# Temporaries placed 64 bytes ahead of the ring's tiles modulo 256, and the cross attention's split keys kept in temporaries

## The chip, the cores and the metric

The kernel runs on one core of a Trainium2 chip. The metric is the device time of one execution in microseconds (us), the median of several. TensorE (PE in the rows, PEld for its weight loads), VectorE (DVE), ScalarE (ACT), GpSimd (POOL) and SyncE (SP) each work through a queue of their own, in the order in which the program was written.

## What is computed

Two transformer-like blocks run one after the other on 256 positions of width 1024, each of depth 2, all in fp32. The part that the change touches by name is the cross attention of the first block:

```python
def memory_cross_attention(x, mem, xa_q, xa_kv, xa_o):
    q = (x @ xa_q).reshape(b, s, XA_HEADS, XA_DIM) * (XA_DIM ** -0.5)   # 4 heads of 256
    k, v = jnp.split(mem @ xa_kv, 2, axis=-1)
    ...
    p = jax.nn.softmax(jnp.einsum('bqhd,bkhd->bhqk', q, k), axis=-1)
    o = jnp.einsum('bhqk,bkhd->bqhd', p, v).reshape(b, s, D_MODEL)
    return o @ xa_o

def first_block(x, mem, ...):
    x = layer_norm(x)
    for l in range(DEPTH):
        x = layer_norm(alpha * x + hybrid_mixer(x, ...))
        x = layer_norm(alpha * x + memory_cross_attention(x, mem, ...))
        x = layer_norm(alpha * x + conv_ffn(x, ...))
```

The hybrid mixer holds a differential attention, a neighbourhood attention and a short convolution; the second block holds two gated feed-forward parts and a mixer with two more attentions, a pooling and a long convolution.

## The kernel before

Each fp32 operand of a large product is split into a high and a low part of type fp32r, and a product is the sum of three matmuls: high by high, high by low, low by high (`mm3`, `half_A`, `group_B`, `run_BK`). Weights come from HBM in pieces of 128 x 1024 by SP's queue into `stg` (5 buffers); ACT casts the high part into `wh` (8 buffers, L313), DVE subtracts the low part into `wl` (7 buffers, L327). Activations stand transposed in `xT`, the memory in `memT`, its keys in `KT`.

Everything that a stage makes goes into one of two pools of tiles with 2048 bytes in each partition: `ring` (23 buffers: split activations, queries, values, gains of the norms) and `tmp` (8 buffers: softmax rows, their transposes, gated products). Each pool hands out its buffers in turn, and the first writer of a buffer waits until all readers of the tile that stood there before are done. The order of instructions on each engine is the order of the Python code (`manual_schedule`); nothing reorders it.

In `cross`, `q(h)` makes the queries of head h with 48 matmuls of 256 columns (`chunk_A`, L392 to L394), splits them into two tiles and splits that head's keys out of `KT` into two more (`split_to`, ACT L522 and DVE L523). Behind it `unit(h)` issues the 12 matmuls of the scores (L1225), the softmax (`attend`, L751 to L790), its transposes (L771), the split of the transposed rows into two temporaries, and the 12 matmuls with the values (L1233):

```python
            t = [[self.ring([128, 2, 256], F32R) for _ in range(2)] for _ in range(2)]
            self.split_to(t[0][0], t[0][1], ps, scale=1.0 / 16.0)
            self.split_to(t[1][0], t[1][1], KT[:, 2 * h:2 * h + 2, :])
```

Where a tile starts inside a partition follows from the pools' order in `__init__`, `first` and `second`. In the built program the start addresses modulo 256 are: `stg`, `wh`, `wl`, `xn`, `ident`, `ring` and `tmp` at 128; `xT`, `memT` and `KT` at 64 (for `memT` and `KT` by the 192 bytes of `gap1` ahead of them). In a row of the trace a matmul's names stand as out<-moving,stationary: `acc<-xT,wh` streams `xT` against weights loaded from `wh`, `tp<-ring,ring` at L1225 streams keys against queries, `tp<-tmp,ring` at L1233 streams softmax rows against values, `tp<-ident,tmp` is a transpose that loads the temporary and streams the identity.

Of the kernel before, what the change touches and what calls it, by code (L numbers as in the profile page):

```python
# [11 lines left out]
F32 = mybir.dt.float32  # L12
F32R = mybir.dt.float32r
# [222 lines left out]
class Gen:  # L236
    def __init__(self, nc, tc, T, ctx):
        self.nc, self.tc, self.T, self.ctx = nc, tc, T, ctx
        P = lambda name, bufs, **k: ctx.enter_context(tc.tile_pool(name=name, bufs=bufs, **k))
        self.p_stg = P("stg", 5)  # L240
        self.p_hl = P("wh", NHL)
        self.p_wl = P("wl", NHL - 1)
        self.p_one = P("one", 1)
        self.p_xT = P("xT", 1)

        P("gap", 1).tile([128, 16], F32, name="gap")
        self.p_ring = P("ring", 23)
        self.p_tmp = P("tmp", 8)
        self.p_sm = P("sm", 24)
        PS = bass.MemoryType.PSUM  # L250
        self.p_acc = P("acc", 4, space=PS)
        self.p_tp = P("tp", 4, space=PS)
        self.used = 0
        self.n = 0
        self.cur = 0
        self.n_dma = 0
        self.n_h = 0
        self.n_l = 0
        self.stg = {}
        self.hl = {}  # L260
        self.lead = 4
        self.floor = None
        self.sides = []
        self.later = []
        self.early = []
# [578 lines left out]
    def first(self, ctx):  # L844
        nc, T = self.nc, self.T
        pf = ctx.enter_context(self.tc.tile_pool(name="first", bufs=1))
        pna = ctx.enter_context(self.tc.tile_pool(name="na", bufs=2))
        pf.tile([128, 48], F32, name="gap1")
        memT = pf.tile([128, 8, 2, 256], F32R, name="memT")
        KT = pf.tile([128, 8, 256], F32, name="KT")  # L850
        make_identity(nc, self.ident)
        nc.gpsimd.memset(self.mhalf, -0.5)
        self.idle_work(WARM)
        mraw = [self.ring([128, 2, 256]) for _ in range(4)]
        for j in range(2):
            nc.scalar.dma_start(mraw[0][:, j, :], T["memT"][:, j, :])
        self.dma_w()
        for k in range(1, 4):
            nc.sync.dma_start(mraw[k], T["memT"][:, 2 * k:2 * k + 2, :])
            self.dma_w()  # L860

        def load_x(t):
            for c in range(2):
                nc.sync.dma_start(self.halves(t)[c], T["x"][t * 128:t * 128 + 128, c * 512:c * 512 + 512])

        load_x(0)
        self.dma_w()
        g0, b0 = self.bcast_rows(T["emb_ln_g"], D, nc.sync), self.bcast_rows(T["emb_ln_b"], D, nc.sync)
        load_x(1)
        self.trig = pf.tile([128, 4, 2, 8], F32, name="trig")  # L870
        self.posf = pf.tile([128, 2], F32, name="posf")
        self.posi = pf.tile([128, 2], I32, name="posi")
        self.memT, self.KT = memT, KT

        nc.vector.tensor_copy(memT[:, 0, 0, :], mraw[0][:, 0, :])
        self.split_h()
        nc.vector.tensor_sub(memT[:, 0, 1, :], mraw[0][:, 0, :], memT[:, 0, 0, :].bitcast(F32))
        self.split_l()
        self.split_to(memT[:, 1, 0, :], memT[:, 1, 1, :], mraw[0][:, 1, :])
        for k in range(1, 4):  # L880
            self.split_to(memT[:, 2 * k:2 * k + 2, 0, :], memT[:, 2 * k:2 * k + 2, 1, :], mraw[k])
            self.pump(k, 0)

        def emb(t):
            list(self.ln_chain(self.halves(t), g0, b0))

        self.lead = 2
        xT = self.new_xT()

        def after(i):  # L890
            if i == 1:
                emb(0)
                nc.sync.dma_start(self.c1, T["c1"])
                nc.sync.dma_start(self.cols, T["cols"])
                self.lamr = self.ring([128, 2, 4, 64])
                nc.sync.dma_start(self.lamr, T["lamr"].partition_broadcast(128))
                nc.sync.dma_start(self.subg, T["subln_g"].partition_broadcast(128))
                nc.sync.dma_start(self.posi, T["pos"])
            if i == 3:
                self.transpose_in(0, self.halves(0), xT)  # L900
                self.lead = 3
            if i == 5:
                emb(1)
                self.lead = 4

        self.xk_first(after)
        tr1 = self.turn1(self.halves(1), xT)
        for l in range(DEPTH):
            xT, tr1 = self.mixer1(l, xT, tr1, pna)
            xT, tr1 = self.cross(l, xT, tr1)  # L910
            if l == 0:
                self.sides.append(self.small_setup2())
            xT, tr1 = self.ffn1(l, xT, tr1)
        return xT, tr1
# [295 lines left out]
    def cross(self, l, xT, tr1):  # L1210
        nc, T = self.nc, self.T
        x = lambda k: xT[:, k, :, :]
        V, KT = [], self.KT
        qT, oT = [], []
        kok = [0, 1, 2, 3] if l == 0 else []

        def unit(h):

            passes = [(a, b, f) for a, b in ((0, 0), (0, 1), (1, 0)) for f in range(2)]

            def A(sc):
                q, k = qT[h]
                for t in range(2):
                    for n, (a, b, f) in enumerate(passes):
                        nc.tensor.matmul(sc[0][:, t, :], q[a][:, f, t * 128:t * 128 + 128], k[b][:, f, :], start=(n == 0),  # L1225
                                         stop=(n == 5))

            def C(PT, o):
                o3 = o.rearrange("p (a b) -> p a b", a=2)
                for f in range(2):  # L1230
                    vc = (h % 2) * 256 + f * 128
                    for n, (a, b, c) in enumerate(passes):
                        nc.tensor.matmul(o3[:, f, :], V[h // 2][c][a][:, vc:vc + 128],  # L1233
                                         PT[0][b][:, c, :, :].rearrange("p a b -> p (a b)"), start=(n == 0), stop=(n == 5))

            def post(o):
                o3 = o.rearrange("p (a b) -> p a b", a=2)
                for f in range(2):
                    p = self.pair()
                    self.split_to(p[:, 0, :], p[:, 1, :], o3[:, f, :])  # L1240
                    oT.append(p)

            return dict(A=A, C=C, post=post, nk=[256, 256], bias=None, norm=self.norm_plain, nb=1, split=True,
                        ready=lambda: len(qT) > h and len(kok) > h, ready_c=lambda: len(vok) > h // 2)

        side = self.attend([unit(h) for h in range(4)])

        self.sides.append(side)
        vok = []

        def q(h):
            ps = self.chunk_A(("A", "xa_q", l, h), x)
            t = [[self.ring([128, 2, 256], F32R) for _ in range(2)] for _ in range(2)]
            self.split_to(t[0][0], t[0][1], ps, scale=1.0 / 16.0)
            self.split_to(t[1][0], t[1][1], KT[:, 2 * h:2 * h + 2, :])
            self.defer(1, lambda: qT.append(t))

        def v(g):
            V.append(self.xv(l, g))
            self.defer(1, lambda: vok.append(g))  # L1260

        if l == 0:
            v(0)
            tr1()
            for h in range(4):
                q(h)
        else:
            self.xk(l, (0, 1), kok)
            tr1()
            q(0)  # L1270
            q(1)
            self.xk(l, (2,), kok)
            q(2)
            v(0)
            self.xk(l, (3,), kok)
            q(3)
        v(1)

        def get(i):
            while len(oT) <= i:  # L1280
                self.step()
            return oT[i]

        return self.ln_end([("BK", "xa_o", l, k) for k in range(4)], get, T["ln_g"][l, 1], T["ln_b"][l, 1])
# [81 lines left out]
    def swiglu(self, l, which, xT, tr1, gap, final=False):  # L1366
# [21 lines left out]
        for j in range(2, NFF):  # L1388
            ps = self.chunk_A(("UG", n, l, j), x, pool=self.acc if j < NFF - 2 else self.tp)
            if j == 2:  # L1390
                first()
            s, p = self.tmp([128, 256]), self.pair()
            nc.scalar.activation(s, ps[:, 1, :], AF.Silu)  # L1393
            nc.vector.tensor_tensor(s, ps[:, 0, :], s, op=ALU.mult)  # L1394
            self.split_to(p[:, 0, :], p[:, 1, :], s)
            hT.append(p)
# [251 lines left out]
```

## Time and profile before

| | |
|---|---|
| median of 3 runs | 2019.42 us (2018.86 to 2019.86) |
| profiled execution, its own time | 2019.2 us |
| its span, first to last instruction | 2017.4 us |
| PE busy | 1995.2 us, 99% |
| PEld busy | 1825.7 us, 90% |
| DVE busy | 1321.1 us, 65% |
| ACT busy | 1094.0 us, 54% |
| POOL busy | 97.1 us, 5% |
| mean granted TensorE clock | 0.997 of full |

Busy time is the union of an engine's instructions. Matmuls overlap in the rows (one begins while the one before is still draining), so the sum of their durations is more than the span; what one matmul costs is the distance from its start to the next start. The 1.8 us between the span and the execution's own time lie outside all instructions.

### The profile page before, as it was taken

The numbers are of one execution on the slowest core, as the hardware profiler recorded it, in microseconds if no ns is written. First come the engines' busy times: TensorE is split into PE (matmuls) and PEld (weight loads), VectorE is DVE, ScalarE is ACT, GpSimd is POOL, SyncE is SP. The second block draws the span as 40 slices with busy tenths as digits, with TensorE's granted clock in tenths as the row PEclk, the third lists the DMA queues.
The fourth block names the chain that finished last, engine by engine and source line by source line (L and its number), as shares of the span: only waits on it lengthen the run. The fifth ranks groups of instructions, "written<-read, shape, count | busy, mean of one in ns | idle before, by whom it ended". The sixth has DMA issues, their size and how long they took to land.

```text
span 2017.4 us, 35071 instructions
## 1 busy us (share of the span) xinstructions
PE 1995.2 (99%) x14178; PEld 1825.7 (90%) x14178; DVE 1321.1 (65%) x2036; ACT 1094.0 (54%) x1806; POOL 97.1 (5%) x142
## 2 busy tenths in 40 slices
PE   9999999999999999999999999999999999999997
PEld 8899989899888999989987998879998998879996
DVE  6776676787577657667766655776555655676553
ACT  5757446465375754546553544575444554575552
POOL 2100000000020000000001000100000000110000
PEclk9999999999999999999999999999999999999999
DMA  8554655466564564645674666555664666445661
GB/s 293 185 165 157 205 194 166 146 216 209 192 204 139 170 212 164 200 156 183 199 245 160 211 197 227 157 161 180 192 228 147 212 195 225 162 153 183 196 224 67
DMA packets 105667, 376.91 MB, mean 187 GB/s; under 512 B 12576, under 2 KB 13088, under 8 KB 105376
## 3 DMA queue, kind: packets, MB, share of 16 engines
q1 hardware_dynamic: 99792, 357.59, 53.5%
q0 software_dynamic: 5136, 16.29, 2.9%
q8 instruction: 111, 1.82, 0.4%
q10 hardware_dynamic: 576, 0.79, 0.1%
q14 instruction: 52, 0.43, 0.1%
HBM read 372.49 MB, written 1.05 MB: 185 GB/s over the span
## 4 chain that ended last, share of the span: by engine, by line
PE 92%; DVE 4%; DMA 1%; issue 1%; ACT 1%; POOL 1%; POOLq 0%; SPq 0%; DVEq 0%; ACTq 0%
PE acc L392 16%; PE acc L394 16%; PE acc L393 16%; PE acc L487 6%; PE acc L485 6%; PE acc L486 6%; PE acc L510 4%; PE acc L430 3%; PE acc L432 3%; PE acc L431 3%; PE acc L452 2%; PE acc L459 1%; PE acc L454 1%; PE tp L392 1%; PE tp L393 1%
## 5 line engine op out<-in xcount | busy, mean ns | idle before, releaser
L327 DVE TENSOR_TENSOR wl<-stg,wh 128x1024 fp32r<-128x1024 f32 (+1 forms) x671 | 801.1, 1221 | 158.6 <-PE acc L486 114.3
L313 ACT CAST wh<-stg 128x1024 fp32r<-128x1024 f32 (+1 forms) x673 | 684.3, 1048 | 180.4 <-PE acc L487 125.1
L392 PE MATMUL acc<-xT,wh 128*128 128x256 f32 x2624 | 729.3, 278 | 0.6 <-ACT xT L604 0.6
L393 PE MATMUL acc<-xT,wh 128*128 128x256 f32 x2624 | 725.2, 276 | 0.8 <-DVE xT L605 0.8
L394 PE MATMUL acc<-xT,wl 128*128 128x256 f32 x2624 | 724.9, 276 | 0.0
L392 PEld LDWEIGHTS acc<-xT,wh 128*128 128x128 f32 x2624 | 492.7, 188 | 3.2 <-ACT xT L604 1.1
L393 PEld LDWEIGHTS acc<-xT,wh 128*128 128x128 f32 x2624 | 493.0, 188 | 1.7 <-DVE xT L605 1.2
L394 PEld LDWEIGHTS acc<-xT,wl 128*128 128x128 f32 x2624 | 492.8, 188 | 0.0
L485 PE MATMUL acc<-wh,ring 128*128 128x512 f32 x528 | 206.7, 391 | 0.7 <-DVE ring L523 0.7
L487 PE MATMUL acc<-wh,ring 128*128 128x512 f32 x528 | 205.8, 390 | 0.2
L486 PE MATMUL acc<-wl,ring 128*128 128x512 f32 x528 | 205.6, 389 | 0.0
L487 PEld LDWEIGHTS acc<-wh,ring 128*128 128x128 f32 x528 | 99.1, 188 | 21.8 <-DVE ring L526 1.1
L485 PEld LDWEIGHTS acc<-wh,ring 128*128 128x128 f32 x528 | 99.2, 188 | 21.5 <-DVE ring L523 1.1
L510 PE MATMUL acc<-wh,ring 128*128 128x512 f32 x384 | 117.5, 394 | 0.0
L486 PEld LDWEIGHTS acc<-wl,ring 128*128 128x128 f32 x528 | 99.2, 188 | 20.0
L1394 DVE TENSOR_TENSOR tmp<-acc,tmp 128x256 f32<-128x256 f32 x72 | 30.5, 424 | 120.8 <-ACT tmp L1393 120.8
L1393 ACT ACTIVATE tmp<-acc 128x256 f32<-128x256 f32 x72 | 27.8, 386 | 148.6 <-PE acc L394 148.6
L522 ACT CAST ring<-tmp 128x256 fp32r<-128x256 f32 x136 | 54.7, 407 | 87.3 <-DVE tmp L1301 42.0
L523 DVE TENSOR_TENSOR ring<-tmp,ring 128x256 fp32r<-128x256 f32 x136 | 57.4, 426 | 64.1 <-ACT ring L522 64.1
L510 PEld LDWEIGHTS acc<-wh,ring 128*128 128x128 f32 x384 | 72.1, 188 | 14.2
L546 POOL TENSOR_TENSOR sm<-sm,mhalf 128x1 f32<-128x1 f32 (+1 forms) x40 | 31.6, 790 | 940.5 <-DVE sm L557 336.1
L430 PE MATMUL acc<-wh,xT 128*128 128x512 f32 (+1 forms) x192 | 74.7, 389 | 0.0
(248 smaller groups left out, 2651.6 us busy)
## 6 DMA issues: line engine op xcount, KB each, us to landing
stg<-in_wpack SPq DMA_DIRECT2D x673, 512.0 KB, 4.1
nab<-in_rpb POOLq DMA_DIRECT2D x8, 384.0 KB, 3.5
ring<-in_ln_g POOLq DMA_DIRECT2D x12, 256.0 KB, 3.9
ring<-in_ln_b POOLq DMA_DIRECT2D x12, 256.0 KB, 5.4
ring<-in_ffn_norm POOLq DMA_DIRECT2D x8, 256.0 KB, 4.3
cst<-hpad POOLq DMA_DIRECT2D x32, 32.9 KB, 4.3
xn<-in_x SPq DMA_DIRECT2D x4, 256.0 KB, 6.4
band<-in_c POOLq DMA_DIRECT2D x1, 1024.0 KB, 5.8
```

Source lines behind the costliest of these rows:

```text
L313: self.nc.scalar.copy((h.bitcast(F32) if f32 else h)[:, c:c + w], self.stg[i][:, c:c + w])
L327: (self.nc.gpsimd if i in POOL_LOW else self.nc.vector).tensor_sub(l[:, w], s[:, w], self.hl[i][0].bitcast(F32)[:, w])
L392: mm(out, lh, rh, start=start, stop=False)
L393: mm(out, lh, rl, start=False, stop=False)
L394: mm(out, ll, rh, start=False, stop=stop)
L430: mm(o, xp[:, 0, ts], h[:, w], start=(i == 0), stop=False)
L431: mm(o, xp[:, 0, ts], l[:, w], start=False, stop=False)
L432: mm(o, xp[:, 1, ts], h[:, w], start=False, stop=(i == n - 1))
L485: mm(b[t][c], xp[:, 0, ts], h[:, w], start=(i == 0), stop=False)
L486: mm(b[t][c], xp[:, 0, ts], l[:, w], start=False, stop=False)
L487: mm(b[t][c], xp[:, 1, ts], h[:, w], start=False, stop=False)
L510: mm(b[tt][cc], xp[:, 1 if kind == "x" else 0, ts], l[:, w] if kind[0] == "l" else h[:, w], start=False, stop=(kind == "x" and i == n - 1))
```

## The change

`gap1`, 192 bytes in the pool `first`, is taken out, and a tile `gap2` of 192 bytes is put between the pools `ring` and `tmp`. In the built program `tmp` then starts at 64 modulo 256 instead of 128; `ring`, `stg`, `wh`, `wl`, `xn`, `ident`, `xT`, `memT` and `KT` stay where they were modulo 256 (`memT` and `KT` to the byte). What stands behind `tmp` in the second block moves by the same 192 bytes: `c2`, `band`, `cln` and `cst` from 128 to 64, `cacc` from 0 to 192. In `cross` the two tiles of split keys of each head come from `tmp` instead of `ring`: 16 tiles in all, two for each of four heads in each of two layers.

```diff
         P("gap", 1).tile([128, 16], F32, name="gap")
         self.p_ring = P("ring", 23)
+
+        P("gap2", 1).tile([128, 48], F32, name="gap2")
         self.p_tmp = P("tmp", 8)
...
-        pf.tile([128, 48], F32, name="gap1")
         memT = pf.tile([128, 8, 2, 256], F32R, name="memT")
...
-            t = [[self.ring([128, 2, 256], F32R) for _ in range(2)] for _ in range(2)]
+            t = [[p([128, 2, 256], F32R) for _ in range(2)] for p in (self.ring, self.tmp)]
```

No instruction is added, removed or moved on any engine. What changes in the order are names: on PE, the scores of the first head of layer 0 read, before (moving, then stationary; the line is that of the matmul):

```order
L394 MATMUL acc_3688<-xT_3322,wl_3579 128x256
L1225 MATMUL tp_3749<-ring_3682,ring_3680 128x256 x2
L1225 MATMUL tp_3749<-ring_3683,ring_3680 128x256 x2
L1225 MATMUL tp_3749<-ring_3682,ring_3681 128x256 x2
L392 MATMUL acc_3770<-xT_3322,wh_3583 128x256
```

and after, with lines one or two higher because of the added lines:

```order
L396 MATMUL acc_3691<-xT_3325,wl_3582 128x256
L1226 MATMUL tp_3752<-tmp_3685,ring_3683 128x256 x2
L1226 MATMUL tp_3752<-tmp_3686,ring_3683 128x256 x2
L1226 MATMUL tp_3752<-tmp_3685,ring_3684 128x256 x2
L394 MATMUL acc_3773<-xT_3325,wh_3586 128x256
```

Only the moving operand is another tile. On ACT, which takes part in filling the temporaries, heads 1 and 2 of the same layer read after the change (`KT` is split, `tp` holds scores):

```order
L524 CAST tmp_664_3767<-KT_110 128x512
L315 CAST wh_669_3778<-stg_645_3625 128x1024
L762 ACT_TABLE_LOAD
L762 ACTIVATE tmp_673_3807,sm_672_3806<-tp_661_3752,sm_671_3805 128x256 x2
L315 CAST wh_676_3816<-stg_648_3655 128x1024
L792 ACTIVATE tmp_673_3807<-tmp_673_3807,sm_677_3842 128x256 x2
L527 ACTIVATE ring_679_3859<-acc_666_3773 128x512
L524 CAST tmp_681_3861<-KT_110 128x512
L315 CAST wh_686_3872<-stg_656_3694 128x1024
L762 ACTIVATE tmp_690_3901,sm_689_3900<-tp_678_3846,sm_688_3899 128x256 x2
L315 CAST wh_694_3915<-stg_659_3724 128x1024
L524 CAST tmp_695_3941<-tp_691_3906 128x512
```

The two casts of `KT` wrote `ring` tiles before; nothing else in these rows is different. With the keys among them, the eight buffers of `tmp` have been handed out once in this layer after the keys of heads 0, 1 and 2 (six tiles) and the softmax rows of heads 0 and 1 (two tiles). The last row, the split of head 0's transposed softmax rows, is the first to take a buffer that held keys, those of head 0; head 3's keys take the buffers of head 1's, and the split rows of head 1 those of head 2's keys.

## Rows read from the trace of the kernel before

**Rows 1.** The span and granted clock, and the page's row of busy times.

```profile
core 0: 2017.4 us, clock 0.997
PE 1995.2 (99%) x14178; PEld 1825.7 (90%) x14178; DVE 1321.1 (65%) x2036; ACT 1094.0 (54%) x1806; POOL 97.1 (5%) x142
```

**Rows 2.** Waits of PE: total us, times, longest; two of twelve rows.

```profile
PE acc L452 <- ACT KT L994: 2.0, 1, 2.0
PE tp L600 <- DVE tmp L582: 1.6, 2, 0.9
```

**Rows 3.** Groups of PE by form: count | busy us, mean ns | idle before.

```profile
L393 PE MATMUL acc<-xT,wh 128*128 128x256 f32 x2624 | 725.2, 276 | 0.8 <-DVE xT L605 0.8
...
L486 PE MATMUL acc<-wl,ring 128*128 128x512 f32 x528 | 205.6, 389 | 0.0
...
L393 PE MATMUL acc<-ring,wh 128*128 128x256 f32 x192 | 54.2, 282 | 0.0
...
L454 PE MATMUL acc<-wl,xT 128*128 128x512 f32 x160 | 40.1, 393 | 0.0
...
L771 PE MATMUL tp<-ident,tmp 128*128 128x128 f32 x176 | 24.5, 273 | 0.9 <-ACT tmp L734 0.9
...
L1233 PE MATMUL tp<-tmp,ring 128*128 128x256 f32 x96 | 12.9, 284 | 0.0
L1225 PE MATMUL tp<-ring,ring 128*128 128x256 f32 x96 | 12.7, 281 | 0.0
...
L431 PE MATMUL acc<-wl,xT 128*128 128x256 f32 x32 | 8.9, 279 | 0.0
...
L1495 PE MATMUL tp<-ident,cacc 128*128 128x128 f32 x8 | 1.5, 272 | 0.0
```

**Rows 4.** Timeline of PE at head 0's scores, layer 0: start us, us.

```profile
308.16 0.28 PE L392 MATMUL acc<-xT,wh 128*128 128x256 f32 x1
...
308.50 0.28 PE L392 MATMUL acc<-xT,wh 128*128 128x256 f32 x1
...
308.73 1.49 PEld L1225 LDWEIGHTS tp<-ring,ring 128*128 128x128 f32 x12
308.84 1.58 PE L1225 MATMUL tp<-ring,ring 128*128 128x256 f32 x12
...
310.26 0.29 PE L392 MATMUL acc<-xT,wh 128*128 128x256 f32 x1
```

**Rows 5.** Timeline of PE in a branch product that streams ring tiles.

```profile
205.94 0.28 PE L392 MATMUL acc<-ring,wh 128*128 128x256 f32 x1
...
207.98 0.28 PE L394 MATMUL acc<-ring,wl 128*128 128x256 f32 x1
```

**Rows 6.** Timeline of PE at head 2's scores, layer 0.

```profile
323.07 1.58 PE L1225 MATMUL tp<-ring,ring 128*128 128x256 f32 x12
324.49 0.39 PE L430 MATMUL acc<-wh,memT 128*128 128x512 f32 x1
```

**Rows 7.** Timeline of ACT in layer 0: head 3's keys, head 1's split rows.

```profile
325.52 0.60 ACT L522 CAST ring<-KT 128x512 fp32r<-128x512 f32 x1
...
331.97 0.59 ACT L522 CAST tmp<-tp 128x512 fp32r<-128x512 f32 x1
```

**Rows 8.** Waits of POOL: one row.

```profile
POOL ring L533 <- PE tp L1225: 75.1, 4, 29.0
```

**Rows 9.** Groups of DVE by form: three that read two tiles.

```profile
L576 DVE TENSOR_TENSOR tmp<-xn,ring 128x512 f32<-128x512 f32 x14 | 9.7, 691 | 0.4
...
L523 DVE TENSOR_TENSOR ring<-KT,ring 128x512 fp32r<-128x512 f32 x8 | 5.5, 682 | 0.0
L523 DVE TENSOR_TENSOR ring<-acc,ring 128x512 fp32r<-128x512 f32 x8 | 5.4, 690 | 8.1 <-ACT ring L522 7.9
```

**Rows 10.** The chain that ended last, at the long convolution and behind it.

```profile
1327.69 3.60 PE acc L1452 x64
1331.29 0.58 PE tp L820 x4
```

## Prediction

> **What bounds the kernel now.** I read the span and the page's busy row first: PE is busy for 1995.2 of 2017.4 us at 0.997 of its clock [rows 1]. The reader is to see that this kernel has no idle bottleneck to fill. The view of PE's waits confirms it: twelve rows, the longest 2.0 us, 11.2 us in all; the largest one that a temporary ends is 1.6 us [rows 2]. So only two kinds of edit can move the time: one that makes PE's own instructions closer or farther apart, or one that makes PE wait where it does not wait now.
>
> Next the groups of PE by form, for what sets a matmul's pace. Two groups of the same line, shape and weights differ only in what they stream: xT takes 276 ns, ring tiles 282 [rows 3]. The starts tell the same in distances. Three matmuls that stream xT lie between 308.16 and 308.50 us, 0.113 us each; twelve score matmuls, ring against ring, run from 308.84 to 310.26 us, 0.118 us each [rows 4]; seventeen that stream ring tiles against weights run from 205.94 to 207.98 us, 0.120 us each [rows 5]. Now lay the start addresses beside it. xT streams from 64 modulo 256 against weights at 128; ring tiles stream from 128 against weights, queries or values at 128. My reading: what is streamed is read while the next weights are being loaded (the first weight load of the scores starts at 308.73 us, beside the matmul before it, [rows 4]); where both reads start at the same place modulo 256 a 256-column matmul costs 5 to 8 ns more than where the stream starts 64 bytes ahead. The opposite order, weights at 64 and a stream at 128, takes 279 ns at 256 columns, and at 512 columns 393 ns against 389 ns for equal places [rows 3]. It is a reading from three relations only; all ring tiles have one place, so pool and place are not told apart by it.
>
> **The change part by part.** *Keys in temporaries at 64, queries in the ring at 128.* The 96 score matmuls (8 heads of 12) get the relation of xT and its weights. Their mean is 281 ns, that of xT 276 [rows 3]: 5 ns x 96 = 0.5 us less. Bounds: nothing, if the place is not the cause, and 8 ns (the largest difference of the group above) x 96 = 0.8 us.
>
> *Softmax rows in temporaries at 64, values in the ring at 128.* The 96 matmuls of L1233 stream a temporary against values: 284 - 276 = 8 ns x 96 = 0.8 us less [rows 3]; bounds nothing and 0.8 us.
>
> *Transposes.* About 376 transposes load a temporary as weights and stream the identity, which stays at 128; they go from equal places to the opposite order, weights at 64. No row shows that at 128 columns in fp32. Nearest: the same transpose with cacc at 0, another relation again, takes 272 ns against 273 for temporaries [rows 3], no difference. Bounds from the opposite order at other widths: +4 ns (393 - 389) and -3 ns (279 - 282) a piece [rows 3], so +1.5 to -1.1 us. I take nothing, by the 272 and 273 ns rows, which are of the same instruction. Ahead of each group of four or more transposes, though, a matmul that streams xT at 64 now overlaps a weight load from a temporary at 64: equal places, up to 7 ns (0.120 - 0.113 us) each. With at most 376/4 = 94 groups that is nothing to 0.7 us; not all follow a matmul on xT, so I take 0.3 us more.
>
> *Other matmuls that touch a moved tile.* The attention products on unsplit softmax rows (L820, 96 instructions in pairs that run beside each other) get the good relation: at most 7 ns x 48 = 0.3 us less. The long convolution streams cst, which moves by 64 too: 64 matmuls in 3.60 us in each layer [rows 10], four beside each other, so 16 rounds x 7 ns = 0.1 us either way, 0.2 us for both. Its taps begin 4 bytes apart, so it passes through many relations already. I take nothing for both; the reading was never seen on instructions that share the array.
>
> *The casts and subtractions of ACT and DVE* read and write tiles at other distances than before. DVE's rows for 512 columns with two tiles at equal places (691 ns), 64 apart (682) and with one input in PSUM (690) agree to 1.3% [rows 9], and both engines have room (65% and 54% busy, [rows 1]). Nothing. If 1% of each operation came back as a longer wait at the few places where PE waits for DVE's or ACT's temporaries, it would be below 0.1 us of the 1.6 us row [rows 2].
>
> *Sixteen more tiles through the eight buffers of tmp.* This adds a condition: a writer of a temporary waits for the scores that read the keys which stood there. Instructions behind it on ACT are the casts of weights, so a late key would starve PE. The tightest case is the split of head 1's transposed rows, which takes the buffers of head 2's keys: those scores have issued by 324.49 us [rows 6], the cast starts at 331.97 us [rows 7], 7.5 us later. Head 3's keys (cast from 325.52 us, [rows 7]) take the buffers of head 1's, whose scores ended at least one chunk of queries (48 matmuls x 0.113 us = 5.4 us) before head 2's: 6.4 us or more. So the wait is over before it is asked: nothing. If that cover were gone, see the rival below.
>
> *Sixteen tiles fewer in the ring.* POOL's loads of the gains of the cross attention's norm stood 75.1 us behind scores [rows 8]. The ring now comes to the places of those tiles later, so these four waits get shorter, each by at most the longest of them, 29.0 us. No row of the view of waits names such a load as what an engine waited for, so they land earlier and lie there; they also cross HBM earlier beside the weights, and no row of PE's waits in this stage names a weight. Nothing.
>
> Sum: -0.5 - 0.8 + 0.3 = -1.0 us, from 2017.4 to 2016.4 us of span, and with the 1.8 us around it 2018.2 us for an execution like the profiled one, which stood 0.2 us under the median of the runs. Against that median, 2019.42 us, it is 2018.4 us.
>
> The Trainium skill (SBUF — State Buffer, "Who interferes with whom") gives TensorE two independent read ports, one for the moving operand and one for weights, and says that it never waits on anyone for SBUF. By that rule equal places cost nothing, and the sum would be the first rival's 2019.4 us. The trace does not agree where one line takes 276 ns on xT and 282 on ring tiles [rows 3]; it leaves open whether the place or something else about the tiles makes the difference.
>
> **The rivals.** *The place is not the cause* (a ring tile is slow for its size or row length, say, and a temporary has the same 2048 bytes). For it: every slow group streams a tile of 2 KB, every fast one a tile of 16 KB. Against it: the opposite order has a third pace, 279 ns, with xT as weights. Then nothing changes: 2019.4 us. Chance 0.16.
>
> *The transposes pay* the 4 ns that the opposite order costs at 512 columns [rows 3], and their groups the whole 0.7 us: -1.3 + 1.5 + 0.7 = +0.9 us, 2020.3 us, slower than before. It decides from (1.3 - 0.7)/376 = 1.6 ns a transpose on. For it: they are four times as many as the matmuls that gain from the keys. Against it: 272 and 273 ns. Chance 0.10.
>
> *A temporary waits for keys.* It begins when scores come more than 7.5 us later than in these rows. Were the scores two chunks of queries later, ACT would stand 2 x 5.4 - 7.5 = 3.3 us, at three heads in each of two layers 20 us if no weights were cast ahead: up to 2039 us. Against it: the order is the same and PE, which sets the scores' time, does not slow down. Chance 0.04.
>
> *All bounds fall on the good side*: -1.6 - 1.1 - 0.3 - 0.2 = -3.2 us, 2016.2 us. Chance 0.05. A gain of over 4 us would need relations outside these rows.
>
> **How the numbers follow.** The forecast, 2018.4 us, has the remaining 0.65. The three runs of before span 1.0 us, so half a microsecond on either side belongs to any of the cases. The range goes from 2016.6 (the better part of the good bounds) to 2020.5 us (the transposes' rival with that spread); outside lie the waiting rival, half of the good one and tails, less than 2 in 10. By 0.2%, 4.0 us, which is about what a measurement of this kernel can tell from no change, all cases but the waiting one are "the same": 0.90. Faster by more: 0.05, for good relations that no row shows. Slower by more: 0.05, the waiting rival and what I have not seen.
>
> **What would show it right or wrong.** In the profile after, the groups of L1225 and L1233 (L1226 and L1234 in the changed listing) at 276 to 277 ns would show the place as cause; unchanged means of 281 and 284 ns the first rival. The group of L771 at 273 ns shows the transposes free, at 277 ns the second rival. Twelve scores should take 1.36 instead of 1.42 us from first start to next. A wait of ACT's L522 (now L524) for scores, when it writes a temporary, would show the third. POOL's 75.1 us should shrink. The forecast is wrong if PE's waits rise above 11.2 us, or if any group of some hundred matmuls that I left at nothing moves by more than 5 ns.

## The result, and the profile after

The changed kernel takes 2028.51 us (median of 6, 2025.21 to 2035.74) against 2019.19 us (2017.52 to 2019.99) for the kernel before on the same chip: a ratio of 1.0051, 95% interval 1.0038 to 1.0065. It is slower by half a per cent, where 2018.4 us was forecast. The kernel before spreads over 2.5 us, the changed one over 10.5 us. The profiled execution of it took 2027.77 us; its span is 2026.0 us, 8.6 us more than before. In the changed listing the lines from 850 on are numbered one higher (L1225 is L1226), those between 248 and 850 two higher (L392 to L394 are L394 to L396).

The span and clock, and the page's row of busy times, which answer to [rows 1]:

```profile
core 0: 2026.0 us, clock 0.997
PE 2005.9 (99%) x14178; PEld 1836.8 (91%) x14178; DVE 1321.1 (65%) x2036; ACT 1094.1 (54%) x1806; POOL 97.9 (5%) x142
```

The same number of instructions on each engine, the same clock, DVE and ACT to 0.1 us as before; PE is 10.7 us busier. PE's waits come to 9.0 us in all, where they were 11.2 us; so nothing of the loss is waiting. The largest of them, and POOL's one on scores (waits: total us, times, longest; answering to [rows 2, 8]):

```profile
PE acc L454 <- ACT KT L995: 2.0, 1, 2.0
PE tp L602 <- DVE tmp L584: 1.6, 2, 0.9
...
POOL ring L535 <- PE tp L1226: 37.0, 2, 18.6
```

The groups of PE by form, changed kernel (count | busy us, mean ns | idle before), answering to [rows 3]:

```profile
L394 PE MATMUL acc<-xT,wh 128*128 128x256 f32 x2624 | 732.8, 279 | 0.6 <-ACT xT L606 0.6
L395 PE MATMUL acc<-xT,wh 128*128 128x256 f32 x2624 | 728.8, 278 | 0.8 <-DVE xT L607 0.8
L396 PE MATMUL acc<-xT,wl 128*128 128x256 f32 x2624 | 728.6, 278 | 0.0
L488 PE MATMUL acc<-wl,ring 128*128 128x512 f32 x528 | 205.6, 389 | 0.0
...
L773 PE MATMUL tp<-ident,tmp 128*128 128x128 f32 x176 | 24.4, 272 | 0.0
...
L1234 PE MATMUL tp<-tmp,ring 128*128 128x256 f32 x96 | 12.7, 282 | 0.0
L1226 PE MATMUL tp<-tmp,ring 128*128 128x256 f32 x96 | 12.4, 279 | 0.0
```

Scores and values gained, less than forecast: 281 to 279 ns and 284 to 282 ns. The transposes did not change (272 ns). The loss stands in the first three rows, the 7872 matmuls that stream xT against the weights: one of them, L395, goes from 276 to 278 ns [rows 3], and its two neighbours move by 1 and 2 ns from what they had before:

```profile
L392 PE MATMUL acc<-xT,wh 128*128 128x256 f32 x2624 | 729.3, 278 | 0.6 <-ACT xT L604 0.6
...
L394 PE MATMUL acc<-xT,wl 128*128 128x256 f32 x2624 | 724.9, 276 | 0.0
```

No operand of theirs was moved. From the starts of all PE instructions in both traces, the distances from such a matmul to the next add up to 9.5 us more than before, and those of the 576 matmuls of the same lines that write `tp` to 0.9 us more; scores and values give back 0.3 and 0.2 us, and all other groups 1.3 us together: +8.5 us, after rounding.

A mean of 278 ns hides two values. The six longest stretches in which PE does nothing but these products (the feed-forward parts, 911 steps each) are cut out here, 100 us from each (window, its us, PE busy of L394 alone, L392 before, and its count, then weight loads, granted clock, DMA's busy share and GB/s). First two of the kernel before, which are like its other four, then the changed one's six:

```profile
389.00:489.00 100.00, 81.18 (x295) 55.20 (x295) 1.00 0.60 198
1571.00:1671.00 100.00, 81.18 (x295) 55.20 (x295) 1.00 0.61 198
```

```profile
388.00:488.00 100.00, 79.52 (x283) 54.34 (x284) 1.00 0.58 192
929.00:1029.00 100.00, 81.18 (x295) 55.20 (x295) 1.00 0.60 198
1118.00:1218.00 100.00, 81.18 (x295) 55.18 (x294) 1.00 0.62 199
1393.00:1493.00 100.00, 81.18 (x295) 55.22 (x295) 1.00 0.61 198
1575.00:1675.00 100.00, 79.52 (x283) 54.34 (x284) 1.00 0.60 193
1854.00:1954.00 100.00, 81.15 (x295) 55.22 (x295) 1.00 0.61 199
```

The reader is to look at the count: 295 matmuls of the line in 100 us, or 283, at a granted clock of 1.00, the 2.4 GHz level, in both. Step by step it is 113.4 ns or 117.9 ns from start to start (a duration of 276 or 281 ns), and a stretch that has taken one pace, within its first ten steps or so, keeps it to its last. Before, all six have 113.4 ns; after, the first and the fifth have 117.9. Each slow one costs 911 x 4.4 ns = 4.0 us. Shorter stretches show the same two paces: of 8377 steps on xT, 450 were at 278.5 ns or more before and 2763 after, (2763 - 450) x 4.44 ns = 10.3 us. That is the loss, before what the other groups give back. Four fifths of it are the two long stretches; the short ones have 931 slow steps where they had 420.

Where the pace is taken shows in PE's timeline at two starts of the changed kernel (start us, us), one slow, one not:

```profile
385.04 0.28 PE L396 MATMUL acc<-xT,wl 128*128 128x256 f32 x1
385.15 0.60 PE L1318 MATMUL tp<-ident,tmp 128*128 128x128 f32 x4
385.51 0.36 PE L394 MATMUL acc<-xT,wh 128*128 128x256 f32 x1
385.71 0.28 PE L395 MATMUL acc<-xT,wh 128*128 128x256 f32 x1
385.83 0.28 PE L396 MATMUL acc<-xT,wl 128*128 128x256 f32 x1
385.95 0.28 PE L394 MATMUL acc<-xT,wh 128*128 128x256 f32 x1
...
927.13 0.60 PE L1318 MATMUL tp<-ident,tmp 128*128 128x128 f32 x4
927.49 0.37 PE L394 MATMUL acc<-xT,wh 128*128 128x256 f32 x1
```

Each of the six begins right behind four transposes of temporaries: these now load from 64 while the identity streams from 128. The same place by groups (only the first matmul of each stretch is in a window of some 0.1 us), at 385.5 and at 927.5 us:

```profile
L394 PE MATMUL acc<-xT,wh 128*128 128x256 f32 x1 | 0.4, 363 | 0.0
...
L394 PE MATMUL acc<-xT,wh 128*128 128x256 f32 x1 | 0.4, 369 | 0.0
```

The first matmul of a slow stretch lasts 363 ns, that of a quick one 369. This mark held in all traces but the one with xT moved, whose stretches have neither pace: 96 long stretches in 16 kernels, of which 13 are slow; those begin with 363 or 364 ns, the other 83 with 365 to 370 ns. It is a mark; that the first matmul causes the pace is not shown.

### The profile page after: what moved, and what is told of

The parts are those of the page before. It is cut to its first block, busy times and chain, and to the rows that moved or that the text cites. A ratio compares the mean times of both kernels' runs of the same rounds, so it can differ in the third digit from the quotient of the medians.

```text
span 2026.0 us, 35069 instructions
## 1 busy us (share of the span) xinstructions
PE 2005.9 (99%) x14178; PEld 1836.8 (91%) x14178; DVE 1321.1 (65%) x2036; ACT 1094.1 (54%) x1806; POOL 97.9 (5%) x142
## 4 chain that ended last, share of the span: by engine, by line
PE 93%; DVE 3%; DMA 1%; issue 1%; ACT 1%; POOL 0%; POOLq 0%; SPq 0%; DVEq 0%; ACTq 0%
PE acc L394 16%; PE acc L395 16%; PE acc L396 16%; PE acc L489 6%; PE acc L487 6%; PE acc L488 6%; PE acc L512 4%; PE acc L432 3%; PE acc L434 3%; PE acc L433 3%; PE acc L454 2%; PE acc L461 1%; PE acc L456 1%; PE tp L395 1%; PE tp L396 1%; PE tp L394 1%
## 5 line engine op out<-in xcount | busy, mean ns | idle before, releaser
L394 PE MATMUL acc<-xT,wh 128*128 128x256 f32 x2624 | 732.8, 279 | 0.6 <-ACT xT L606 0.6
L395 PE MATMUL acc<-xT,wh 128*128 128x256 f32 x2624 | 728.8, 278 | 0.8 <-DVE xT L607 0.8
L396 PE MATMUL acc<-xT,wl 128*128 128x256 f32 x2624 | 728.6, 278 | 0.0
L394 PEld LDWEIGHTS acc<-xT,wh 128*128 128x128 f32 x2624 | 495.2, 189 | 3.2 <-ACT xT L606 1.1
L395 PEld LDWEIGHTS acc<-xT,wh 128*128 128x128 f32 x2624 | 492.9, 188 | 1.7 <-DVE xT L607 1.2
L396 PEld LDWEIGHTS acc<-xT,wl 128*128 128x128 f32 x2624 | 493.2, 188 | 0.0
```

What stands on the lines that cost most here:

```text
L394: mm(out, lh, rh, start=start, stop=False)
L395: mm(out, lh, rl, start=False, stop=False)
L396: mm(out, ll, rh, start=False, stop=stop)
```

## The experiments

*Start theory*: the transposes at a stretch's start, now with unequal places of what is loaded and what streams, decide the pace of everything behind them. *Keys theory*: the other order in which ring and temporaries are handed out does it. *Traffic theory*: ACT and DVE, which now read and write temporaries at xT's place, slow the matmuls on xT. "Long runs" in the expectations are the six stretches. Ratios are to the kernel before on the same chip (its medians there are 2018.5 to 2018.8 us). The counts of slow stretches and slow steps are of one traced execution of each kernel.

### The change in its parts

Keys in temporaries, all places as before:

```diff
-t = [[self.ring([128, 2, 256], F32R) for _ in range(2)] for _ in range(2)]
+t = [[p([128, 2, 256], F32R) for _ in range(2)] for p in (self.ring, self.tmp)]
```

> The kernel before with the split keys in temporaries and all tiles at the old places (temporaries at 128 modulo 256). Start theory (a long run of 256-column matmuls keeps one of two paces, 113.3 or 117.8 ns, decided at its start by the transposes of temporaries just ahead of it, and temporaries at 64 make the slow pace likelier): nothing moves, 2018 to 2020 us, all six runs of 911 matmuls at 276 ns each. Keys theory (the other use of the buffers of tmp brings the slow pace): 2024 to 2036 us, some of the six runs at 281 ns.

Measured: 2018.83 us, ratio 1.0003 (0.9994 to 1.0012); all six stretches quick, scores at 282 ns, values at 284. The keys theory falls for the long stretches. In the short ones slow steps do rise, from 450 to 683 in all (1.0 us), though every place is as before; the time does not show it.

The places alone: the changed kernel with that line as it was before.

> The changed kernel with the split keys back in the ring; temporaries at 64 modulo 256. Start theory: like the changed kernel, 2024 to 2036 us, one to four of the six long runs at 281 ns a matmul. Keys theory: 2018 to 2020 us, none slow. Scores (queries and keys both at 128) back at 281 ns under both.

Measured: 2026.14 us (2025.2 to 2032.9), ratio 1.0044 (1.0028 to 1.006); three of six stretches slow, 3661 slow steps. The loss is in the places.

The changed kernel with the identity moved to 64 too, so that the transposes of temporaries load and stream at equal places again (those of xn, at 128, no longer do); the temporaries stay at 64:

```diff
+one.tile([128, 48], F32, name="gap3")
 self.ident = one.tile([128, 128], F32, name="ident")
 ...
 self.c1 = one.tile([128, 208], F32, name="c1")[:, :200]
+one.tile([128, 16], F32, name="gap4")
```

> The changed kernel with the identity moved to 64 modulo 256 as well, so that a transpose again loads and streams from equal places, as before the change; temporaries stay at 64. Start theory: all six long runs at 276 ns, 2017 to 2020 us. Traffic theory (reads and writes of temporaries by the other engines at 64 collide with xT, which streams from 64): still slow, 2024 to 2036 us.

Measured: 2018.06 us, ratio 0.9997 (0.9988 to 1.0007); all six quick, 482 slow steps. Its groups by form:

```profile
L1236 PE MATMUL tp<-tmp,ring 128*128 128x256 f32 x96 | 12.7, 282 | 0.0
L1228 PE MATMUL tp<-tmp,ring 128*128 128x256 f32 x96 | 12.3, 277 | 0.0
```

The traffic theory falls, since ACT and DVE use temporaries at 64 as in the changed kernel. The tiles that moved along behind `tmp` (`c2`, `band` and the like) are not the cause either: here they lie as in the changed kernel, too. This is the changed kernel without its loss, and with scores at 277 ns, within the 276 to 277 ns that the forecast gave them; the values stay at 282 ns.

A fourth place, temporaries at 192 (64 bytes behind the ring's):

```diff
-P("gap2", 1).tile([128, 48], F32, name="gap2")
+P("gap2", 1).tile([128, 16], F32, name="gap2")
 ...
+pf.tile([128, 32], F32, name="gap1")
```

> The changed kernel with temporaries at 192 modulo 256 instead of 64: 64 bytes behind the ring, and the identity at 128 streams from 64 bytes ahead of a temporary. Start theory: the transposes have the relation that xT has to its weights, the long runs start fast, 2017 to 2020 us; values and softmax rows (moving 64 behind) stay near 279 to 284 ns. Traffic theory: no traffic at xT's place, also 2017 to 2020 us. If any place but 128 disturbs the start, 2024 to 2036 us.

Measured: 2021.25 us, ratio 1.0011 (1.0001 to 1.002); long stretches quick, but 1099 slow steps, nearly all in short ones. The long stretches are as the start theory has it, but the time lies in neither branch of the expectation. Unequal places on the other side seem to lose too, less; the interval all but reaches 1.

### Is it the transposes just ahead?

Four more transposes behind the real ones at each of the six starts, into a bank that nobody reads. In the kernel before, they load xT (64) or, as a control, xn (128); in the changed kernel they load xn.

```diff
+def spare(self, f):
+    p = self.p_tp.tile([128, 512], F32, tag="tp", name=self.nm("tp"))
+    for j in range(4):
+        self.nc.tensor.transpose(p[:, j * 128:j * 128 + 128], f(j), self.ident)
 ...
+self.spare(lambda j: xT[:, j, 0, :128].bitcast(F32))
```

> The kernel before, with four transposes more at each of the six places where a run of 911 matmuls of 256 columns begins, right behind the transposes of the temporaries: they load a block of xT (64 bytes from the temporaries' places modulo 256, as the temporaries lie in the changed kernel), stream the identity from 128 and fill a spare bank that nobody reads. The temporaries stay where they were. 24 transposes of about 0.09 us each cost 2.2 us by themselves. Start theory (the transposes just ahead of a run, by the places of their two operands, decide its pace): one to four of the six long runs take 117.9 ns a step, 4.0 us for each, so 2025 to 2037 us. Rival (it is the temporaries' place as such, through whoever reads or writes them): all six at 113.4 ns, 2021.4 us.

Measured: 2025.80 us (2024.49 to 2026.23), ratio 1.0034 (1.0021 to 1.0047); the fifth stretch slow, the others quick. Windows of L392, columns as above:

```profile
1391.00:1491.00 100.00, 81.18 (x295) 55.22 (x295) 1.00 0.59 197
1573.00:1673.00 100.00, 79.52 (x283) 54.34 (x284) 1.00 0.58 192
```

> The control of the run with xT: the same four transposes more at the same six places, but they load a block of xn, which lies at 128 modulo 256 as the identity does. Both theories: all six long runs at 113.4 ns and 2021.4 us. If long runs are slow here too, four more transposes as such upset the start, whatever they load, and the start theory has lost its reason in places.

Measured: 2020.96 us, ratio 1.0010 (1.0 to 1.0019); all six quick. So 4.8 us of the run with xT, a little over the price of one slow stretch, come from what the extra transposes load, xT at 64 and not xn at 128; no temporary was moved.

> The changed kernel, temporaries at 64, with the four transposes more of xn (128) behind those of the temporaries at the six places, so that the last thing ahead of a long run loads and streams at equal places again. Start theory, if the last transposes decide: all six long runs at 113.4 ns; of the 10.3 us lost in slow steps the short runs' 2.3 us stay, and with 2.2 us for the transposes it is 2023 us (2021 to 2025). Start theory, if a pace once upset by the earlier transposes stays: 2030.7 us with slow long runs. Rival (place of the temporaries as such): 2030.7 us too, but it falls if the long runs are all at 113.4 ns.

Measured: 2037.68 us (2035.94 to 2039.48), ratio 1.0095 (1.008 to 1.011); four of six slow. Equal places in the last four transposes repair nothing. This missed the first branch of the expectation, and, 7 us above its 2030.7 us, the second too: the added transposes made it worse.

The identity alone at 64 in the kernel before, temporaries at 128:

> The kernel before with the identity alone moved to 64 modulo 256; temporaries and everything else stay at 128. If unequal places of the loaded and the streamed operand upset the start, some runs are at the slow pace: 2022 to 2034 us. If only a loaded tile at 64 ahead of the streamed one does it, the paces are those of before: 2019 us; then also the transposes themselves, which stream 64 bytes ahead of what they load, may gain by up to some 3 ns each (800 of them: 2.4 us).

Measured: 2023.76 us (2019.74 to 2028.21), ratio 1.0024 (1.0015 to 1.0034). The profiled execution is one of the quicker ones, 2020.53 us, with all six stretches quick and 940 slow steps. Its transposes of temporaries take 273 ns, as before, so they gained nothing. Unequal places in either order lose time; in which stretches the longer executions lost it was not recorded.

Only two buffers at another place than the other temporaries, for the tiles transposed at the six starts (`nat`, L1311 and L1375 of the changed kernel; the expectation numbers them one higher), either way round, keys in the ring:

```diff
+self.p_nat = P("nat", 2)
 P("gap2", 1).tile([128, 48], F32, name="gap2")
-self.p_tmp = P("tmp", 8)
+self.p_tmp = P("tmp", 6)
```

> The changed kernel with the keys back in the ring and, of the eight temporary buffers, two apart at 128 modulo 256 for the tiles that are transposed at the start of the six long runs (lines 1312 and 1376); the other six stay at 64. All other places as in the changed kernel. Start theory (the transposes at a run's start, by the places of what they load, upset its pace): all six long runs at 113.4 ns a step, the short runs as in the changed kernel, so about 2021 us (2019 to 2023). Rival (any work on temporaries at 64, wherever it is, slows some runs): one to three long runs slow, 2024 to 2033 us.

Measured: 2020.93 us, ratio 1.0010 (1.0 to 1.002); six quick, 1013 slow steps in short stretches. As the start theory has it.

> The mirror of the run with two buffers at 128: six temporaries at 128, as in the kernel before, and only the two for the tiles transposed at the start of the six long runs at 64; all other places as in the changed kernel. Start theory: one to three of the six long runs at 117.9 ns, 4.0 us each: 2022 to 2031 us, while the short runs that no such transpose precedes keep their paces. Rival (any work on temporaries at 64): 2019 us, all six long runs at 113.4 ns, as the other six buffers carry nearly all the work.

Measured: 2020.24 us (2019.27 to 2023.91), ratio 1.0009 (1.0 to 1.0019); six quick, 704 slow steps. The start theory expected one to three slow and fails: unequal transposes stand ahead of all six stretches, and none is slow in this trace (one of the ten executions, without a trace, took 2023.91 us). The rival, which failed in the run before this one, expected this one rightly. A rule of places at the start is not enough.

### Is the place the cause of a pace at all?

xT moved to 128, the weights' place, in the kernel before:

```diff
-self.p_xT = P("xT", 1)
 P("gap", 1).tile([128, 16], F32, name="gap")
+self.p_xT = P("xT", 1)
```

> The kernel before with xT alone moved from 64 to 128 modulo 256, where the stored weights lie: the 64 bytes of padding stand ahead of xT and not behind it. What it tells: whether the two paces belong to the 64 bytes between the streamed and the loaded operand. If they do (the slow pace is that of equal places, and 64 bytes apart a run can get the fast one), all 8377 steps go at the slow pace or slower, 113.4 to 117.9 ns, 37 us over the kernel before, 2056 us or more. If the two paces are whatever the places are: fast long runs with 276 ns rows remain, and the time is within 2015 to 2035 us.

Measured: 2071.2 us (one execution), all stretches at 120.1 ns a step. Groups by form:

```profile
L391 PE MATMUL acc<-xT,wh 128*128 128x256 f32 x2624 | 746.3, 284 | 0.6 <-ACT xT L603 0.6
L392 PE MATMUL acc<-xT,wh 128*128 128x256 f32 x2624 | 742.6, 283 | 0.8 <-DVE xT L604 0.8
L393 PE MATMUL acc<-xT,wl 128*128 128x256 f32 x2624 | 742.5, 283 | 0.0
...
L430 PE MATMUL acc<-wl,xT 128*128 128x256 f32 x32 | 9.0, 283 | 0.0
```

Same tile, same size, same rows, 64 bytes on: 283 ns and 52 us more. Equal places have a third pace of their own here, slower than both. The last row tells place and relation apart: there xT is what is loaded, and the weights that stream against it stayed at 128; they go from 279 ns (L431 in [rows 3]) to 283 all the same. So the place of a streamed tile by itself does not set the pace; that of the loaded one counts too.

### The moment of the start

One and two equal-place transposes of xn at the six starts, which move no place, only what stands ahead of a stretch and with it the moment of its start (the edit is against the helper shown above, here for two):

```diff
-    for j in range(4):
+    for j in range(2):
```

> The changed kernel with one transpose of xn (equal places, 128 and 128) behind those of the temporaries at the start of each of the six long runs; own cost 6 x 0.11 us = 0.7 us. Moment theory (the few ns at which a run starts pick its pace, and places only shift them): another number of slow long runs than the two of the changed kernel and the four with four such transposes, in no order; time 2020 + 4 us for each slow one. Place theory (the unequal transposes ahead upset the start, an equal one does nothing): two to four slow ones, about 2029 to 2037 us, as without it.

Measured: 2021.17 us (2020.13 to 2022.91), ratio 1.0014 (1.0003 to 1.0026); none of six slow, 847 slow steps. As the moment theory has it; the place theory expected two to four.

> As the run with one transpose of xn in the changed kernel, with two; own cost 1.3 us. Moment theory: the number of slow long runs differs from that with one, and need not lie between those with none and with four; 2021 us + 4 us for each slow one. Place theory: 2030 to 2038 us with two to four slow ones.

Measured: 2033.82 us (two executions, 0.05 us apart), ratio 1.0075 (1.0046 to 1.0105); three slow, which both theories allow. Windows of L394:

```profile
389.00:489.00 100.00, 81.14 (x295) 55.22 (x295) 1.00 0.60 197
926.00:1026.00 100.00, 81.15 (x295) 55.22 (x295) 1.00 0.59 196
1116.00:1216.00 100.00, 79.52 (x283) 53.13 (x284) 1.00 0.58 191
1395.00:1495.00 100.00, 81.18 (x295) 55.22 (x295) 1.00 0.60 196
1577.00:1677.00 100.00, 79.53 (x284) 53.12 (x283) 1.00 0.59 192
1856.00:1956.00 100.00, 79.53 (x284) 53.12 (x283) 1.00 0.59 193
```

> The kernel before, temporaries at 128, with one transpose of xn behind those of the temporaries at the start of each long run; own cost 0.7 us. Moment theory in its strict form (any shift of the start's moment draws anew, whatever the places): slow long runs appear here too, 2020 us + 4 us for each. Place theory: none, 2019.5 us; four such transposes already gave none.

> As the run with one transpose of xn in the kernel before, with two; own cost 1.3 us. Strict moment theory: slow long runs in one of the two, 2024 us or more. Place theory: none in either, 2020.2 us. If neither has any, equal places ahead of a run are enough for the fast pace whatever the moment, and unequal ones leave it open.

Measured: 2018.71 us, ratio 0.9996 (0.9985 to 1.0008), and 2019.50 us, 1.0003 (0.9992 to 1.0014); no slow stretch in either, 442 and 432 slow steps, as the place theory has it. In the changed kernel 0, 1, 2 and 4 such transposes give 2, 0, 3 and 4 slow stretches, in the kernel before always none. The times bear out the 0 and the 4: all eight executions with one transpose (at most 2022.91 us) are quicker than all six of the changed kernel (2025.21 to 2035.74 us), and all four with four at each start are slower (2035.94 us or more, of which the transposes themselves are some 2.6 us). The two executions with two lie within the changed kernel's range, so 3 against 2 may be chance. So neither theory holds alone: where places are unequal, the number of transposes ahead changes how many stretches are slow, and not in step; where they are equal, no number tried made a slow stretch in a trace. That it acts through the moment is argued, not shown, since each added transpose also changes what stands ahead. Nor is a slow stretch at equal places ruled out: one of 21 executions of the kernel before beside these runs took 2023.16 us, 4.4 us over their median, about the price of one, and no trace of it is kept.

The slow steps account for the spans to within 2 us. The worked column is 2017.4 + (slow steps - 450) x 4.44 ns + 0.11 us for each added transpose (109 ns from one to the next):

| kernel | slow stretches | slow steps | worked, us | span, us |
|---|---|---|---|---|
| changed | 2 | 2763 | 2027.7 | 2026.0 |
| places alone | 3 | 3661 | 2031.7 | 2031.1 |
| identity at 64 too | 0 | 482 | 2017.5 | 2015.9 |
| before, xT spare | 1 | 1432 | 2024.4 | 2024.0 |
| before, xn spare | 0 | 510 | 2020.3 | 2019.4 |
| changed, 4 xn spare | 4 | 4612 | 2038.5 | 2037.7 |
| changed, 2 xn spare | 3 | 3648 | 2032.9 | 2032.1 |
| changed, 1 xn spare | 0 | 847 | 2019.8 | 2018.6 |

Worked lies above measured by 0.4 to 1.7 us in every row, and by 0.4 to 1.3 us in the seven other kernels with the two paces. A part of that is the starting point: the trace of the kernel before is of an execution of 2019.2 us, 0.4 to 0.7 us over the medians beside the experiments. The gains of scores and values are another part in some rows; the rest stays open.

## Why the prediction was wrong

**The bound** was read rightly: PE had no idle time to lose or win, and all of the 8.6 us is its own instructions farther apart.

**The place as cause** was right, and the first rival wrong: with xT at 128 its matmuls take 283 ns; the scores take 282 with keys in temporaries at 128, and 277 with keys in temporaries at 64 and equal-place transposes. The Trainium skill (SBUF — State Buffer, "Who interferes with whom") says that TensorE reads through two independent ports and waits on nobody. The measurement does not agree with ports that are independent, and it decides: 64 bytes in xT's place are worth 52 us of 2019. Whether the two reads meet, as the prediction's reading has it, no trace shows.

**The step that failed** is the sentence on what stands beside the transposes: a matmul that streams xT now overlaps the load of a temporary at equal places, "up to 7 ns ... each. With at most 376/4 = 94 groups that is nothing to 0.7 us". It charged one matmul for each group and put all others on xT at nothing, taking their pace as fixed by their own operands' places. In fact two paces are open to the same operands, and a stretch keeps the one that it has after its first steps: what was priced at 7 ns a group costs up to 911 x 4.4 ns = 4.0 us, and 2313 steps more at the slow pace cost 10.3 us where 0.3 us was put. Without that (identity moved too) the kernel takes 2018.06 us, within 0.4 us of the forecast; in part by luck: the kernel before took 2018.77 us beside that run, so the gain is 0.7 us and not 1.0, in an interval that holds no change.

**Scores and values**: mechanism right, sizes wrong. -0.5 us measured -0.3 (12.7 to 12.4 us busy, [rows 3]), and -0.8 us measured -0.2 (12.9 to 12.7). Groups of twelve have the two paces as well: in the changed kernel 41 of the scores' matmuls last 276 ns and 49 last 281, of the values' 24 and 68. So the relation of xT and its weights does not bring xT's 276 ns with it, which the sum took for granted.

**Transposes at nothing** for themselves (272 against 273 ns), **no wait on a temporary**, **POOL's loads earlier** (75.1 to 37.0 us; no wait of PE names them) and **nothing on DVE and ACT** all came as forecast. The transposes of temporaries by the identity are 392 in the trace and not about 376; the bound of 0.7 us stays.

**The alarm was set in the wrong unit.** I wrote that the forecast is wrong if a group left at nothing moves by more than 5 ns. The group that undid it moved by 1 to 2 ns in the mean, with 7872 members. The 0.05 for slower held only one named mechanism, and not this one.

What stays open: why a stretch keeps its pace, what the 1 ns between 364 and 365 ns at its start is made of, what picks the pace, and why unequal places in the transposes ahead bear on it. The traces give starts and ends to 1 ns and nothing of the reads behind them.

## What to carry to other kernels

Before taking a group's time as fixed because its own operands do not move, split it by stretch: a mean can hide two paces, and then a cheap neighbour at the start can be worth the whole stretch behind it. Weigh a change of places by the largest group that stands next to it, not by the instructions that it touches, and try equal places of what is loaded and what streams in the transposes ahead of long products: where the transposes of temporaries and the added ones had them, none of 36 stretches in six traced kernels was slow; where some had not, 13 of 54 in nine. The run with two buffers at 128, equal only just ahead of the stretches, had none of six. All these are versions of one kernel, traced once each.

## What was not expected of the hardware

A row of matmuls on unchanged operands, at a granted clock of 1.00, runs at 113.4 or 117.9 ns a step and stays there for 911 steps; it is not pulled back. Which of the two it will be shows within a few ns at the start (363 to 364 ns of the first matmul against 365 to 370). So adding work can help: the changed kernel with six useless transposes is 7 us faster than without them (2021.17 against 2028.51 us), and with 24 it is 9 us slower (2037.68 us). No version tried is measurably faster than the kernel before; the lowest ratios are 0.9996 (0.9985 to 1.0008), with one transpose of xn more at each start in the kernel before, and 0.9997 (0.9988 to 1.0007), with temporaries and identity at 64.
